# Recurrent units of a long mixed kernel take their buffers in two stages, and the gated branch runs in two threads

## The chip, the cores and the metric

The kernel runs on one core of a Trainium2 chip. Times are device microseconds (us) of one execution. A profile is one execution recorded by the hardware; its stretches and instructions are counted in us from the start of its span. The core has five instruction queues that matter here: TensorE (PE), VectorE (DVE), ScalarE (ACT), GpSimd (POOL), and SyncE (SP), which issues most transfers. Each works through its own instructions in the order in which the program holds them and waits where one of them needs a result of another engine.

## The reference, cut to what matters

Two blocks follow each other on a sequence of 1024 tokens with 1024 channels. The first is a two-layer transformer (pooling, sliding-window attention, two feed-forward networks). The second, which the change touches, computes

```
h = x*(1+scale) + shift;  p = h @ w_in                      # 29 column tiles of 128
out_a = u * (causal w_spatial @ layer_norm(v) + b) * silu(gate)   # per chunk of 128 tokens
r, k, v, w, a = token-shifted columns of p                  # 8 heads of 64
for t: S = S*w_t + (S a_t) b_t^T + v_t k_t^T;  y_t = S r_t  # RWKV-7
out_b = (group_norm(y) + bonus) * silu(gate)
x = layer_norm(ALPHA*x + gate*(concat(out_a, out_b) @ w_out))
```

## The kernel before, in words

Everything is FP32 in effect: a GEMM is done in three passes over a high and a low part (helper at L265, so every matmul has that line, and every transpose L269). The sequence is cut in two halves, h=0 and h=1. The program is written by generators ("threads") that a small planner runs: `yield 6000` lets other threads go on until a planned clock has moved on by that many ns, `("ev", x)` waits for an event, `("acq", pool, n)` for n buffers of a count. The planner's order is TensorE's order, word for word. On the other engines a scheduler orders the instructions by that order and by priorities.

The second block runs once for each half. While h=0 runs, the second feed-forward network of h=1 fills TensorE. In h=1 nothing else is left. `second` (L1384) makes 29 input GEMMs: one for the decay inputs (`wdad`), then k, r, v for four pairs of heads (`pk`, `pr`, `pv`), four gates (`pg`), and twelve for the gated branch (`pgv`, `pgu`, `pgg`). Their results take turns in four banks; ScalarE and VectorE copy each away, and it goes to memory.

A recurrent unit `rwkv(p, h)` (L1072) handles pair p of heads. Its names on TensorE, in order, are: `zw`, `za`, `kt`, `kn` (decays and norms of k), `A` (products inside chunks of 64, masked by VectorE into `Aa` and `W`), `bt`, `vt`, `bn`, `F`; then VectorE solves 16-by-16 triangles in 15 pairs of small instructions (L1182, L1183), with transfers through memory before (`nd`, `Dm`) and after (`ud`, `td`); then `P1`, `T3`, `U3`, `P2`, `U6` (larger triangles), `GH`, `QM`, eight steps of `S` (the state, one step after the other by way of ScalarE), `y`, and `yo` (transposes after the norm). In names as `zw2_1` the first digit is p and the second h. All small products share four more PSUM banks.

Buffers of 528 columns come from a pool of 67, counted by `T`. A unit takes 15 before it starts, gives 4 back after `GH`, 10 after `y`, and takes 3 for the norm. Two units can be under way at once in h=1. The gated branch (`gmlp`, L1012: `gc`, `gt`, `gp`) does its four blocks one after the other in one thread. `out_first` (L1420) projects h=0 (`po2`) and then normalizes it in its own thread of low priority by `final` (L1569: `mean0`, the squares' sum `sql0`, `st_ln0`, `sb_ln0`). `out_second` (L1447) projects h=1 in two halves of columns; its first three pieces (`po24`, `po26`, `po27`) do seven of the eight inputs before it needs unit 3.

Of the kernel before, what the change touches and what calls it, by code (L numbers as in the profile page):

```python
# [19 lines left out]
T = 1024  # L20
# [12 lines left out]
NT = 67  # L33
# [150 lines left out]
class K:  # L184
# [824 lines left out]
        nc.sync.dma_start(out=self.gd[h][which, m], in_=t)  # L1009
        self.events.add(n2)  # L1010

    def gmlp(self, h):  # L1012

        nc, rp = self.nc, self.rp
        for m in range(4):
            nm = f"{m}_{h}"
            yield ("ev", f"gv{m}{h}")
            yield ("ev", f"gu{m}{h}")
            yield ("ev", f"gg{m}{h}")

            wsp = rp.tile([128, 2, 128], F32, tag="wsp", name=f"wsp{nm}", bufs=1)
            self.load(wsp.rearrange("p e t -> p (e t)"), self.A["wsp"][:, 256 * m:256 * m + 256])
            nc.vector.tensor_tensor(out=wsp, in0=wsp, in1=self.caus.unsqueeze(1).to_broadcast([128, 2, 128]), op=ALU.mult)
            yield 6000
            pc = self.pss(f"gc{nm}")
            for e in range(2):
                self.mm(pc[64 * e:64 * e + 64, :128], self.ones[:, :64], wsp[:, e])
            C = rp.tile([128, 128], F32, tag="gC", name=f"gC{nm}", bufs=1)
            for e in range(2):
                self.load(C[64 * e:64 * e + 64, :], self.A["bsp"][2 * m + e:2 * m + e + 1, :].to_broadcast([64, 128]))  # L1030
            nc.vector.scalar_tensor_tensor(out=C, in0=pc[:, :128], scalar=self.v("lnv_b", m), in1=C, op0=ALU.mult, op1=ALU.add)
            yield ("acq", "TG"[h], 5)
# [12 lines left out]
            nc.vector.tensor_tensor(out=x3, in0=pv, in1=sm.unsqueeze(2).to_broadcast([128, 8, 64]), op=ALU.add)
            sq = self.tt(f"gq{nm}")
            nc.scalar.activation(out=sq, in_=xc, func=AF.Square)
            sm2 = self.tiny("gs2", f"gs2{nm}")
            nc.vector.reduce_sum(out=sm2, in_=sq.rearrange("p (a d) -> p a d", d=64), axis=AX.X)
            nc.vector.tensor_scalar(out=sm2, in0=sm2, scalar1=1.0 / 64, scalar2=LN_EPS, op0=ALU.mult, op1=ALU.add)  # L1050
            rs = self.tiny("gr", f"gr{nm}")
            nc.gpsimd.tensor_tensor(out=rs, in0=sm2, in1=self.nhalf[:, :8], op=ALU.pow)
            nc.gpsimd.tensor_tensor(out=x3, in0=x3, in1=rs.unsqueeze(2).to_broadcast([128, 8, 64]), op=ALU.mult)
            yield 17000
            po = self.pss(f"gp{nm}")
            for j in range(4):
                for e in range(2):
                    self.mm(po[64 * e:64 * e + 64, 128 * j:128 * j + 128], xc[:, 128 * j + 64 * e:128 * j + 64 * e + 64], wsp[:, e])
            t = self.tt(f"gw{nm}")
            nc.vector.scalar_tensor_tensor(out=t.rearrange("p (a b) -> p a b", b=128), in0=po.rearrange("p (a b) -> p a b", b=128),  # L1060
                                           scalar=self.v("lnv_g", m), in1=C.unsqueeze(1).to_broadcast([128, 4, 128]), op0=ALU.mult, op1=ALU.add)
            for x in (0, 2):
                u = self.tt(f"gl{nm}_{x}")
                self.after(nc.sync.dma_start(out=u, in_=self.gd[h][x, m]))
                nc.vector.scalar_tensor_tensor(out=t, in0=u, scalar=0.5 if x else 1.0, in1=t, op0=ALU.mult, op1=ALU.mult)
            nc.sync.dma_start(out=self.od[h][m], in_=t)
            yield 6000
            self.res["TG"[h]] += 5
            self.events.add(f"od{m}_{h}")
            yield 0  # L1070

    def rwkv(self, p, h):  # L1072
# [8 lines left out]
        yield ("ev", f"rk{nm}")  # L1081
        if h:
            yield ("ev", f"st{p}")
        yield ("acq", "early", 1)
        yield ("acq", "T", 15)
        k, r, v, wd = tl("k"), tl("r"), tl("v"), tl("wd")
        for t, m in ((wd, 16), (k, 4 + p), (r, p), (v, 8 + p)):
            self.after(nc.sync.dma_start(out=t, in_=self.qd[h][m]))
# [32 lines left out]
            self.tp(pn[:, 128 * j:128 * j + 128], sq[:, 128 * j:128 * j + 128])  # L1121
        kk = sq
        nc.vector.scalar_tensor_tensor(out=kk, in0=k, scalar=self.v("k_k", p), in1=pn, op0=ALU.mult, op1=ALU.mult)
        yield ("acq", "AR", 1)
        AR = rp.tile([128, 2, 512], F32, tag="AR", name=f"AR{nm}", bufs=3)
        BK = [tl(f"BK{par}_", 4, 2, 64) for par in range(2)]
        E3, k3 = c64(E), c64(kk)
        Aa3 = c64(AR[:, 0])
        nc.vector.scalar_tensor_tensor(out=Aa3[:, :, 1:64], in0=k3[:, :, 1:64], scalar=-1.0, in1=E3[:, :, 0:63], op0=ALU.mult, op1=ALU.mult)
        nc.vector.tensor_scalar(out=Aa3[:, :, 0:1], in0=k3[:, :, 0:1], scalar1=-1.0, scalar2=None, op0=ALU.mult)  # L1130
        nc.gpsimd.tensor_tensor(out=AR[:, 1], in0=r, in1=E, op=ALU.mult)
# [17 lines left out]
        Wc = lambda e, c: W[e][c // 4][:, c % 4]  # L1149
        ms = self.m64[:, 0:64].unsqueeze(1)  # L1150
        mi = self.m64[:, 64:128].unsqueeze(1)
        A4 = AR.rearrange("p s (c t) -> p s c t", t=64)
        for g in range(2):
            pq = [self.pss(f"A{nm}_{g}{e}") for e in range(2)]
            for e in range(2):
                for j in range(4):
                    c = 4 * g + j
                    pe = slice(64 * e, 64 * e + 64)
                    self.mm(pq[e][:, 128 * j:128 * j + 128], BK[c % 2][pe, c // 2].rearrange("p s t -> p (s t)"), A4[pe, :, c])
            for e, ps in enumerate(pq):  # L1160
                p4 = ps.rearrange("p (c r x) -> p r c x", r=2, x=128)
                for par in range(2):
# [124 lines left out]
        for g in range(2):  # L1287
# [8 lines left out]
            for par in range(2):  # L1296
                b = slice(64 * par, 64 * par + 64)
                for j in range(2):
                    nc.vector.tensor_copy(HV[par][b, hi(par, 2 * g + j)], p4[b, j, :, 64:128])
        self.res["T"] += 4  # L1300
        yield 2200

        QM = [tl(f"QM{par}_", 4, 128) for par in range(2)]
        for par in range(2):
# [3 lines left out]
            for cp in range(4):  # L1308
                for e in range(2):
                    self.mm(p3[64 * e:64 * e + 64, cp], G[b, cp, e], Wc(e, 2 * cp + par)[b])  # L1310
            nc.vector.tensor_tensor(out=QM[par][:, :, 0:64], in0=p3[:, :, 0:64], in1=pc(AR[:, 1])[:, :, par], op=ALU.add)
            nc.vector.tensor_tensor(out=QM[par][:, :, 64:128], in0=p3[:, :, 64:128], in1=self.m64[:, 192:256].unsqueeze(1).to_broadcast([128, 4, 64]), op=ALU.add)
        yield 1500

# [24 lines left out]
        for c in range(8):  # L1339
# [4 lines left out]
            for e in range(2):  # L1344
                pe = slice(64 * e, 64 * e + 64)
                self.mm(py[e][b, 64 * cp:64 * cp + 64], QM[par][pe, cp, 0:64], S[pe, c], False, True)
        self.res["T"] += 10
        self.res["S"] += 1
        self.res["AR"] += 1

        yield ("acq", "T", 3)
        y8 = self.tiny("y8", f"y8{nm}").rearrange("p (c e) -> p c e", e=2)
        yt = self.tt(f"yt{nm}")
        y4 = yt.rearrange("p (c e i) -> p c e i", e=2, i=64)
# [26 lines left out]
        self.res["T"] += 4  # L1381
        self.events.add(f"od{4 + p}_{h}")

    def second(self, h, X):  # L1384
        yield ("ev", f"x{X['name']}_0")
        if h:
            self.res["T"] += 14
            self.res["G"] = 5
        yield from self.shifted(16, h, X, f"wdad{h}")
        self.spawn(self.gmlp(h))  # L1390
        for p in range(4):
            self.spawn(self.rwkv(p, h), 2 - 0.01 * (4 * h + p))
            for n2, m in (("k", 4 + p), ("r", p), ("v", 8 + p)):
                yield from self.shifted(m, h, X, f"{n2}{p}{h}")
            self.events.add(f"rk{p}_{h}")
        for p in range(4):
            yield from self.shifted(12 + p, h, X, f"g{p}{h}")
            self.events.add(f"rg{p}_{h}")
        for x, m in ((1, 0), (0, 0), (2, 0), (1, 1), (0, 1), (2, 1), (1, 2), (0, 2), (2, 2), (1, 3), (0, 3), (2, 3)):
            yield from self.gmlp_gemm(x, m, h, X)  # L1400
        self.res["T"] += 16


    def cut(self, t, name):
# [12 lines left out]
    def out_first(self):  # L1417
# [259 lines left out]
```

## Time and profile before

| | |
|---|---|
| three runs | 2799.4, 2804.0 (median), 2806.66 us |
| the profiled execution | 2798.96 us, span 2797.2 us |
| TensorE busy | 2612.4 us, 93% of the span |
| VectorE, ScalarE, GpSimd busy | 1585.8, 1067.2, 347.0 us |
| mean granted clock of TensorE | 0.957 |

The granted clock says which part of its full 2.4 GHz TensorE ran at; 0.5 is the low level of 1.2 GHz. Busy time that overlaps between engines is no sum of the span. A wait names the instruction that was waited for.

### The profile page before, as it was taken

The page shows a single profiled execution, that of the slowest core. Times are in us where ns is not written, and L with a number is a line of the kernel's source. Part 1 is how long each engine was busy: PE and PEld are TensorE (multiplying, and loading weights), DVE is VectorE, ACT ScalarE, POOL GpSimd, SP SyncE. Part 2 cuts the span into 40 slices and gives each one's busy share as a digit, 9 for nine tenths or more (in the row PEclk, how much of TensorE's full clock was granted, in tenths as well). Part 3 has the DMA queues.
Part 4 walks back from the last instruction along what each step waited for, and adds up shares of the span by engine and source line. Part 5 has one row for each costly group of instructions (what it writes and reads, how often), then busy time and mean ns, then how long its engine had stood idle before and what let it go on. Part 6 is the DMA issues. An engine that isn't in the chain of part 4 may idle for free. (4 is left out here: it accounts for less than half of the span.)

```text
span 2797.2 us, 41641 instructions
## 1 busy us (share of the span) xinstructions
PE 2612.4 (93%) x16381; PEld 2172.6 (78%) x16381; DVE 1585.8 (57%) x3092; ACT 1067.2 (38%) x2009; POOL 347.0 (12%) x324
## 2 busy tenths in 40 slices
PE   5999999999999999999999999999999999997476
PEld 4988999888878877887888778777777777775366
DVE  6546654664665366545654655356675465645734
ACT  5333322354554333444543343333222234333223
POOL 3103000300000023000002111011020012104213
PEclk8999999999999999999999999999999999997668
DMA  4465343333222344222224344433233245432222
GB/s 148 131 144 174 129 136 91 128 116 101 90 74 76 106 147 130 92 96 81 81 87 128 114 137 136 134 103 117 86 100 100 96 144 178 126 128 90 86 71 68
DMA packets 183508, 314.57 MB, mean 112 GB/s; under 512 B 44792, under 2 KB 99498, under 8 KB 183312
## 3 DMA queue, kind: packets, MB, share of 16 engines
q1 hardware_dynamic: 174416, 296.06, 33.1%
q10 hardware_dynamic: 8896, 15.84, 2.4%
q8 instruction: 129, 2.11, 0.3%
q14 instruction: 67, 0.55, 0.1%
HBM read 266.60 MB, written 45.23 MB: 111 GB/s over the span
## 5 line engine op out<-in xcount | busy, mean ns | idle before, releaser
L265 PE MATMUL pda0A<-hha0A,wh_da0A 128*128 128x264 f32 x352 | 103.3, 293 | 10.9 <-ACT acca0A L646 6.8
L265 PE MATMUL po<-oc,wh_wo 128*128 128x256 f32 (+1 forms) x384 | 96.1, 344 | 13.1 <-ACT oc L1408 11.1
L265 PE MATMUL pga0A<-xh_a0A,wh_ga0A 128*128 128x264 f32 x352 | 102.9, 292 | 3.7 <-ACT xh_a0A L438 2.5
L265 PE MATMUL pda0A<-hla0A,wh_da0A 128*128 128x264 f32 x352 | 102.5, 291 | 1.0 <-DVE hla0A L637 1.0
L265 PE MATMUL pga0A<-xl_a0A,wh_ga0A 128*128 128x264 f32 x352 | 101.9, 289 | 0.5 <-DVE xl_a0A L439 0.5
L265 PE MATMUL pda0A<-hha0A,wl_da0A 128*128 128x264 f32 x352 | 102.3, 291 | 0.0
L265 PE MATMUL pua0A<-xh_a0A,wh_ua0A 128*128 128x264 f32 x352 | 102.2, 290 | 0.0
L265 PE MATMUL pua0A<-xh_a0A,wl_ua0A 128*128 128x264 f32 x352 | 101.4, 288 | 0.0
L265 PE MATMUL pua0A<-xl_a0A,wh_ua0A 128*128 128x264 f32 x352 | 101.4, 288 | 0.0
L265 PE MATMUL pga0A<-xh_a0A,wl_ga0A 128*128 128x264 f32 x352 | 101.4, 288 | 0.0
L392 POOL TENSOR_TENSOR sqo<-sqo,sq 128x512 f32<-128x512 f32 x4 | 5.2, 1294 | 743.7 <-ACT sq L391 743.7
L265 PEld LDWEIGHTS po<-oc,wh_wo 128*128 128x128 f32 x384 | 69.8, 207 | 21.9 <-ACT oc L1408 12.0
L817 ACT ACTIVATE l<-l,anm 128x256 f32<-128x256 f32 x128 | 63.5, 497 | 54.5 <-DVE anm L809 54.5
L265 PEld LDWEIGHTS pda0A<-hha0A,wh_da0A 128*128 128x128 f32 x352 | 68.7, 195 | 13.4 <-ACT acca0A L646 7.1
L265 PE MATMUL pda1B<-hha1B,wh_da1B 128*128 128x512 f32 x176 | 73.4, 417 | 3.4 <-DVE fg L632 2.4
L265 PE MATMUL pga1A<-xh_a1A,wh_ga1A 128*128 128x512 f32 x176 | 70.9, 403 | 2.2 <-ACT xh_a1A L464 2.2
L265 PE MATMUL pua1B<-xh_a1B,wh_ua1B 128*128 128x512 f32 x176 | 72.2, 410 | 0.0
L265 PE MATMUL pga1B<-xh_a1B,wh_ga1B 128*128 128x512 f32 x176 | 71.3, 405 | 0.8 <-ACT xh_a1B L464 0.6
L265 PE MATMUL pga1B<-xl_a1B,wh_ga1B 128*128 128x512 f32 x176 | 70.4, 400 | 1.7 <-DVE xl_a1B L465 1.7
L265 PEld LDWEIGHTS pga0A<-xh_a0A,wh_ga0A 128*128 128x128 f32 x352 | 67.8, 193 | 5.2 <-ACT xh_a0A L438 3.0
L265 PE MATMUL pda1A<-hha1A,wh_da1A 128*128 128x512 f32 x176 | 70.6, 401 | 1.1 <-ACT hha1A L636 1.1
L265 PE MATMUL pga1A<-xl_a1A,wh_ga1A 128*128 128x512 f32 x176 | 70.0, 398 | 1.6 <-DVE xl_a1A L465 1.6
(798 smaller groups left out, 8303.0 us busy)
## 6 DMA issues: line engine op xcount, KB each, us to landing
ada<-in_w_ada_dram ACTq DMA_DIRECT2D x24, 512.0 KB, 3.6
wr_ga0A<-in_wgu_dram SPq DMA_DIRECT2D x22, 512.0 KB, 4.1
wr_ua0A<-in_wgu_dram SPq DMA_DIRECT2D x22, 512.0 KB, 4.6
wr_da0A<-in_wdn_dram SPq DMA_DIRECT2D x22, 512.0 KB, 3.7
wr_ga0B<-in_wgu_dram SPq DMA_DIRECT2D x22, 512.0 KB, 3.5
wr_ua0B<-in_wgu_dram SPq DMA_DIRECT2D x22, 512.0 KB, 3.5
wr_da0B<-in_wdn_dram SPq DMA_DIRECT2D x22, 512.0 KB
wr_ga1A<-in_wgu_dram SPq DMA_DIRECT2D x22, 512.0 KB, 3.5
```

Source lines behind the costliest of these rows:

```text
L265: self.last = self.nc.tensor.matmul(out, lhsT, rhs, start=start, stop=stop).ins
L392: (eng or nc.gpsimd).tensor_tensor(out=acc[:, :w], in0=acc[:, :w], in1=sq[:, :w], op=ALU.add)
L817: nc.scalar.activation(out=lf[:, x], in_=lf[:, x], func=AF.Exp, bias=nm4[:, x:x + 1], accum_out=den[:, x:x + 1])
```

## The change

A unit now takes 10 buffers before it starts, 5 more when its triangles begin, gives 5 back after `GH`, 7 after `y`, and keeps 3 for the norm (given back at its end); there is no third wait for buffers. Its array `AR` is two tiles (halves of the sequence), so that the masks' inputs are written, multiplied and added by halves; there are six such tiles for three units, and unit 3 of h=1 takes its two from the pool of 67 instead. The pool's counts are larger in h=1. The gated branch keeps its two constant arrays in one buffer of the pool, and in h=1 its blocks 0, 2 and 1, 3 run in two threads. The gates' GEMMs (`pg`) no longer precede the gated branch's but alternate with them. The first half's last norm is a thread of its own with the usual priority.

```diff
-    def gmlp(self, h):
+    def gmlp(self, h, ms=range(4)):
...
-            wsp = rp.tile([128, 2, 128], F32, tag="wsp", name=f"wsp{nm}", bufs=1)
+            yield ("acq", "TG"[h], 6)
+            wc = self.ht(f"wsp{nm}")
+            wsp = wc[:, :256].rearrange("p (e t) -> p e t", e=2)
...
+        own = h == 1 and p == 3
         yield ("acq", "early", 1)
-        yield ("acq", "T", 15)
+        yield ("acq", "T", 12 if own else 10)
...
+            yield ("acq", "AR", 1)
+            AR = [rp.tile([128, 2, 4, 64], F32, tag="AR", name=f"AR{g}_{nm}", bufs=6) for g in range(2)]
...
+        yield ("acq", "T", 5)
         Un, Tn = tl("U"), tl("T")
...
-        self.res["T"] += 4
+        self.res["T"] += 5
...
-        self.res["T"] += 10
+        self.res["T"] += 9 if own else 7
...
-        yield ("acq", "T", 3)
...
         if h:
-            self.res["T"] += 14
-            self.res["G"] = 5
+            self.res["T"] += NT - 41
+            self.res["G"] = 6
...
-        self.spawn(self.gmlp(h))
+        if h:
+            for e in range(2):
+                self.spawn(self.gmlp(h, range(e, 4, 2)))
+        else:
+            self.spawn(self.gmlp(h))
...
         for p in range(4):
+            for x in (1, 0, 2):
+                yield from self.gmlp_gemm(x, p, h, X)
             yield from self.shifted(12 + p, h, X, f"g{p}{h}")
...
-        for x, m in ((1, 0), (0, 0), (2, 0), (1, 1), (0, 1), (2, 1), (1, 2), (0, 2), (2, 2), (1, 3), (0, 3), (2, 3)):
-            yield from self.gmlp_gemm(x, m, h, X)
-        self.res["T"] += 16
+        if h:
+            self.res["T"] += 10
+            self.res["G"] += 6
+        else:
+            self.res["T"] += 16
...
-        yield from self.final(y, 0, 512, ysum)
-        self.res["T"] += 12
+        self.spawn(self.final(y, 0, 512, ysum, 12))
```

TensorE, where unit 2 of h=1 starts. Before, `zw2_1` stands after unit 0's `yo`, with one GEMM (`pgg31`, the last of the 29) still to come:

```order
L265 MATMUL QM1_1_1_22739<-W00_1_1_21714,T1_1_21751 64x128
...
L269 MATMUL yo0_1_22750<-eye_75,yt0_1_22634 128x128 x4
L265 MATMUL zw2_1_22761<-wd2_1_22680,wup2_1_22685 128x512
L265 MATMUL za2_1_22762<-wd2_1_22680,wup2_1_22685 128x512
L269 MATMUL kt2_1_22781<-eye_75,kq2_1_22687 128x128 x4
...
L265 MATMUL gc1_1_22800<-wsp1_1_22689,ones_76 64x128 x2
L265 MATMUL pgg31_22818<-xh_b1B_0_0_20496,wh_gg31_22813 128x512
...
L269 MATMUL kn2_1_22849<-eye_75,kq2_1_22687 128x128 x4
```

Now it stands right after unit 1's `F`, among unit 0's triangles:

```order
L265 MATMUL F1_1_1_21947<-HV1_1_1_21930,Aa1_1_1_21808 64x64 x2
...
L265 MATMUL zw2_1_22076<-wd2_1_21972,wup2_1_21977 128x512
L265 MATMUL za2_1_22077<-wd2_1_21972,wup2_1_21977 128x512
L269 MATMUL kt2_1_22096<-eye_75,kq2_1_21979 128x128 x4
L265 MATMUL P20_1_22107<-T0_1_21401,Aa0_0_1_21362 32x32
...
L265 MATMUL gc0_1_22126<-wsp0_1_21985,ones_76 64x128 x2
L265 MATMUL pgv11_22148<-xh_b1B_0_0_20516,wh_gv11_22143 128x512
...
L265 MATMUL U60_1_22173<-U0_1_21400,N0_1_21571 32x32 x16
L269 MATMUL kn2_1_22192<-eye_75,kq2_1_21979 128x128 x4
```

Unit 2 moved from behind the 28th GEMM to behind the 17th; between its `kt` and `kn` there are `P2`, `gc`, one GEMM and `U6`.

TensorE, at the end of h=1. Before, unit 3's `P1` follows unit 2's `y`, and pieces of the output projection (`po2`) lie between unit 3's stages:

```order
L265 MATMUL S2_1_7_23763<-S2_1_23701,QM1_2_1_23669 64x64 x2
L265 MATMUL y2_1_0_23769<-HV0_2_1_23092,W00_2_1_22960 64x64
...
L265 MATMUL P13_1_23819<-T3_1_23395,N3_1_23572 64x64 x16
L265 MATMUL gp3_1_23838<-wsp3_1_23631,gx3_1_23729 64x128 x8
L265 MATMUL T33_1_23856<-P3_1_23836,U3_1_23394 64x64 x16
...
L265 MATMUL GH3_1_1_24043<-F1_3_1_23492,U3_1_23394 64x128 x8
L265 MATMUL po24_1_0_24066<-oc00_1_22895,wh_wo24_1_23966 128x256
...
L265 MATMUL QM3_1_0_24090<-W00_3_1_23358,T3_1_23395 64x128
...
L265 MATMUL po26_1_0_24112<-oc00_1_22895,wh_wo26_1_23972 128x256
...
L265 MATMUL S3_1_0_24136<-HV0_3_1_23478,W00_3_1_23358 64x64
...
L265 MATMUL y3_1_0_24206<-HV0_3_1_23478,W00_3_1_23358 64x64
...
L269 MATMUL yo3_1_24256<-eye_75,yt3_1_24241 128x128 x4
```

Now unit 3's `P1` comes one step after the last GEMM (`pg31`), beside unit 2's `S`:

```order
L265 MATMUL pg31_23659<-xh_b1B_0_0_20516,wh_g31_23654 128x512
...
L265 MATMUL S2_1_0_23686<-HV0_2_1_22494,W00_2_1_22360 64x64
...
L265 MATMUL P13_1_23692<-T3_1_23039,N3_1_23292 64x64 x16
L265 MATMUL S2_1_1_23734<-HV1_2_1_22495,W00_2_1_22360 64x64
...
L265 MATMUL T33_1_23740<-P3_1_23709,U3_1_23038 64x64 x16
...
L265 MATMUL GH3_1_1_23902<-F1_3_1_23136,U3_1_23038 64x128 x8
...
L265 MATMUL y2_1_0_23928<-HV0_2_1_22494,W00_2_1_22360 64x64
...
L265 MATMUL QM3_1_0_23980<-W00_3_1_22988,T3_1_23039 64x128
...
L265 MATMUL S3_1_0_24006<-HV0_3_1_23122,W00_3_1_22988 64x64
...
L265 MATMUL y3_1_0_24171<-HV0_3_1_23122,W00_3_1_22988 64x64
...
L265 MATMUL po24_1_0_24230<-oc00_1_23724,wh_wo24_1_24102 128x256
...
L269 MATMUL yo3_1_24296<-eye_75,yt3_1_24206 128x128 x4
```

The pieces of the output projection moved behind unit 3's `y`.

VectorE, the first half's last norm. Before, its subtractions and its sum of squares stand among the masks of unit 2 (`Aa`, `W`):

```order
L1008 SCALAR_TENSOR_TENSOR sgg31_22889<-sgg31_22889,pgg31_22818 128x512
...
L1579 TENSOR_TENSOR yo20_0_20506<-yo20_0_20506,mean0_22901 128x512
...
L1579 TENSOR_TENSOR yo26_0_20789<-yo26_0_20789,mean0_22901 128x512
L1163 TENSOR_TENSOR Aa0_2_1_22958<-A2_1_00_22964,m64_14001 128x128
...
L1164 TENSOR_TENSOR W00_2_1_22960<-A2_1_00_22964,m64_14001 128x4x64
L392 TENSOR_TENSOR sql0_22903<-sql0_22903,sq_22931 128x512
L1163 TENSOR_TENSOR Aa0_2_1_22958<-A2_1_01_22965,m64_14001 128x128
```

Now they stand in front of the first copies of h=1's GEMM results (`shwdad1`, `shk01`):

```order
L330 TENSOR_TENSOR wl_v01_21006<-wr_v01_21004,wh_v01_21005 128x1024
L1593 TENSOR_TENSOR yo20_0_20526<-yo20_0_20526,mean0_20893 128x512
...
L1593 TENSOR_TENSOR yo26_0_20809<-yo26_0_20809,mean0_20893 128x512
L392 TENSOR_TENSOR sql0_20895<-sql0_20895,sq_20923 128x512
L985 SCALAR_TENSOR_TENSOR shwdad1_20926<-pwdad1_20866,vecs_74,shwdad1_20926 128x511
L987 TENSOR_TENSOR shwdad1_20926<-shwdad1_20926,shp_14011 128x1
L985 SCALAR_TENSOR_TENSOR shk01_20963<-pk01_20938,vecs_74,shk01_20963 128x511
```

The sum of squares, which waits for GpSimd, moved out of unit 2 and ahead of the units altogether.

## Rows read from the trace of the kernel before

**Rows 1.** The page's head, and its row of the granted clock in 40 slices.

```profile
span 2797.2 us, 41641 instructions
...
PEclk8999999999999999999999999999999999997668
```

**Rows 2.** Two stretches of h=1: length, busy time by engine (instructions), clock, DMA.

```profile
core 0: us, PE busy (x) PEld busy (x) DVE busy (x) ACT busy (x) POOL busy (x), PEclk, DMA share, GB/s
2327.45:2541.25 213.80, 212.39 (x1515) 167.78 (x1515) 116.44 (x269) 78.22 (x121) 27.50 (x27) 1.00 0.42 134
2541.25:2731.80 190.55, 112.30 (x1165) 87.94 (x1165) 96.97 (x246) 51.48 (x104) 45.34 (x40) 0.66 0.25 76
```

**Rows 3.** Stretches: A to F; F; P; P2; T, U; GH; QM; y; S step.

```profile
2385.32:2391.16 5.84, 5.84 (x53) 4.86 (x53) 3.35 (x14) 2.20 (x6) 2.02 (x2) 1.00 0.06 7
2396.89:2398.01 1.12, 1.12 (x33) 1.05 (x32) 0.00 (x0) 0.59 (x1) 0.00 (x0) 1.00 0.86 310
2436.01:2437.26 1.25, 1.25 (x33) 1.19 (x32) 0.31 (x1) 0.00 (x0) 0.60 (x1) 1.00 0.29 32
2451.61:2452.23 0.62, 0.62 (x34) 0.58 (x33) 0.62 (x2) 0.62 (x1) 0.00 (x0) 1.00 0.00 0
2494.71:2496.67 1.96, 1.96 (x68) 1.89 (x66) 0.69 (x1) 0.53 (x2) 0.99 (x1) 1.00 0.43 146
2464.37:2466.26 1.89, 1.89 (x33) 1.72 (x33) 1.03 (x3) 0.98 (x2) 0.00 (x0) 1.00 0.20 18
2472.01:2473.53 1.52, 1.52 (x33) 1.35 (x32) 0.00 (x0) 0.03 (x1) 0.00 (x0) 1.00 0.99 383
2518.17:2523.02 4.85, 4.85 (x64) 3.84 (x63) 0.00 (x0) 0.00 (x0) 0.00 (x0) 1.00 0.95 321
2479.66:2480.19 0.53, 0.53 (x10) 0.40 (x9) 0.00 (x0) 0.42 (x1) 0.00 (x0) 1.00 0.86 224
```

**Rows 4.** Timeline of TensorE at zw to kn of unit 1.

```profile
2403.77 0.69 PE L265 MATMUL zw<-wd,wup 64*128 64x512 f32 x1
...
2404.83 0.65 PE L269 MATMUL kt<-eye,kq 128*128 128x128 f32 x4
2405.24 0.48 PE L265 MATMUL pv<-xh_b1B,wh_v 128*128 128x512 f32 x1
...
2417.91 0.63 PE L269 MATMUL kn<-eye,kq 128*128 128x128 f32 x4 [1.30 <-DVE kq L1117]
```

**Rows 5.** Waits of TensorE from 2541 to 2732: us in total, times, longest.

```profile
PE S L265 <- DVE QM L1312: 6.9, 2, 5.0
...
PE bt L269 <- DVE W L1164: 3.4, 1, 3.4
```

**Rows 6.** Stretches at a gap before the first half's output projection.

```profile
2272.00:2276.00 4.00, 0.30 (x2) 0.00 (x0) 2.56 (x5) 2.58 (x4) 1.26 (x1) 0.93 1.04 394
2276.00:2286.00 10.00, 8.38 (x23) 6.66 (x24) 6.58 (x12) 3.75 (x8) 1.94 (x1) 0.52 0.27 104
```

**Rows 7.** Timeline of TensorE: P and yo of unit 3, output projection.

```profile
2670.47 0.37 PE L265 MATMUL P<-T,N 64*64 64x64 f32 x1
...
2722.33 1.08 PE L269 MATMUL yo<-eye,yt 128*128 128x128 f32 x4 [5.83 <-DVE yt L1368]
2731.81 1.31 PE L265 MATMUL po<-oc,wh_wo 128*128 128x256 f32 x2 [8.40 <-ACT oc L1408]
```

**Rows 8.** Stretches of the output projection's first three pieces alone.

```profile
2684.28:2692.87 8.59, 5.43 (x21) 4.22 (x21) 0.00 (x0) 0.00 (x0) 0.70 0.62 238
2695.70:2699.72 4.02, 4.02 (x21) 3.88 (x21) 0.00 (x0) 0.00 (x0) 0.63 0.70 235
2702.16:2706.34 4.18, 4.18 (x21) 4.04 (x21) 0.00 (x0) 0.00 (x0) 0.60 0.00 0
```

**Rows 9.** Timeline of VectorE among unit 2's masks.

```profile
2570.86 0.69 DVE L392 TENSOR_TENSOR sql<-sql,sq 128x512 f32<-128x512 f32 x1 [13.53 <-POOL sql L392]
```

More of the change, by code (lines that the diff above doesn't have):

```diff
@@ L1010, in gmlp_gemm @@
         self.events.add(n2)
-    def gmlp(self, h):
-        nc, rp = self.nc, self.rp
-        for m in range(4):
+    def gmlp(self, h, ms=range(4)):
+        nc = self.nc
+        for m in ms:
             nm = f"{m}_{h}"
@@ L1027, in gmlp @@
                 self.mm(pc[64 * e:64 * e + 64, :128], self.ones[:, :64], wsp[:, e])
-            C = rp.tile([128, 128], F32, tag="gC", name=f"gC{nm}", bufs=1)
+            C = wc[:, 256:384]
             for e in range(2):
@@ L1031, in gmlp @@
             nc.vector.scalar_tensor_tensor(out=C, in0=pc[:, :128], scalar=self.v("lnv_b", m), in1=C, op0=ALU.mult, op1=ALU.add)
-            yield ("acq", "TG"[h], 5)
             x = self.tt(f"gv{nm}")
@@ L1067, in gmlp @@
             yield 6000
-            self.res["TG"[h]] += 5
+            self.res["TG"[h]] += 6
             self.events.add(f"od{m}_{h}")
@@ L1123, in rwkv @@
         nc.vector.scalar_tensor_tensor(out=kk, in0=k, scalar=self.v("k_k", p), in1=pn, op0=ALU.mult, op1=ALU.mult)
-        yield ("acq", "AR", 1)
-        AR = rp.tile([128, 2, 512], F32, tag="AR", name=f"AR{nm}", bufs=3)
+        if own:
+            AR = [tl(f"AR{g}_", 2, 4, 64) for g in range(2)]
+        else:
+            yield ("acq", "AR", 1)
+            AR = [rp.tile([128, 2, 4, 64], F32, tag="AR", name=f"AR{g}_{nm}", bufs=6) for g in range(2)]
         BK = [tl(f"BK{par}_", 4, 2, 64) for par in range(2)]
         E3, k3 = c64(E), c64(kk)
[L1128 to L1131, printed above, removed]
+        for g in range(2):
+            c = slice(4 * g, 4 * g + 4)
+            nc.vector.scalar_tensor_tensor(out=AR[g][:, 0, :, 1:64], in0=k3[:, c, 1:64], scalar=-1.0, in1=E3[:, c, 0:63], op0=ALU.mult, op1=ALU.mult)
+            nc.vector.tensor_scalar(out=AR[g][:, 0, :, 0:1], in0=k3[:, c, 0:1], scalar1=-1.0, scalar2=None, op0=ALU.mult)
+            nc.gpsimd.tensor_tensor(out=AR[g][:, 1], in0=c64(r)[:, c], in1=E3[:, c], op=ALU.mult)
         pcol = rp.tile([128, 8], F32, tag="pcol", name=f"pcol{nm}", bufs=3)
@@ L1151, in rwkv @@
         mi = self.m64[:, 64:128].unsqueeze(1)
-        A4 = AR.rearrange("p s (c t) -> p s c t", t=64)
         for g in range(2):
@@ L1158, in rwkv @@
                     pe = slice(64 * e, 64 * e + 64)
-                    self.mm(pq[e][:, 128 * j:128 * j + 128], BK[c % 2][pe, c // 2].rearrange("p s t -> p (s t)"), A4[pe, :, c])
+                    self.mm(pq[e][:, 128 * j:128 * j + 128], BK[c % 2][pe, c // 2].rearrange("p s t -> p (s t)"), AR[g][pe, :, j])
             for e, ps in enumerate(pq):
@@ L1225, in rwkv @@
             for j in range(2):
-                self.tp(p4[:, j, :, 0:64], AR[:, 0, 128 * (2 * g + j):128 * (2 * g + j) + 128])
+                self.tp(p4[:, j, :, 0:64], AR[g][:, 0, 2 * j:2 * j + 2].rearrange("p c t -> p (c t)"))
             pf.append((ps, p4))
@@ L1310, in rwkv @@
                     self.mm(p3[64 * e:64 * e + 64, cp], G[b, cp, e], Wc(e, 2 * cp + par)[b])
-            nc.vector.tensor_tensor(out=QM[par][:, :, 0:64], in0=p3[:, :, 0:64], in1=pc(AR[:, 1])[:, :, par], op=ALU.add)
+            for g in range(2):
+                c = slice(2 * g, 2 * g + 2)
+                nc.vector.tensor_tensor(out=QM[par][:, c, 0:64], in0=p3[:, c, 0:64], in1=AR[g][:, 1, par::2], op=ALU.add)
             nc.vector.tensor_tensor(out=QM[par][:, :, 64:128], in0=p3[:, :, 64:128], in1=self.m64[:, 192:256].unsqueeze(1).to_broadcast([128, 4, 64]), op=ALU.add)
@@ L1346, in rwkv @@
                 self.mm(py[e][b, 64 * cp:64 * cp + 64], QM[par][pe, cp, 0:64], S[pe, c], False, True)
-        self.res["T"] += 10
+        self.res["T"] += 9 if own else 7
         self.res["S"] += 1
-        self.res["AR"] += 1
-        yield ("acq", "T", 3)
+        self.res["AR"] += not own
         y8 = self.tiny("y8", f"y8{nm}").rearrange("p (c e) -> p c e", e=2)
@@ L1380, in rwkv @@
         yield 6000
-        self.res["T"] += 4
+        self.res["T"] += 3
         self.events.add(f"od{4 + p}_{h}")
@@ L1396, in second @@
         for p in range(4):
+            for x in (1, 0, 2):
+                yield from self.gmlp_gemm(x, p, h, X)
             yield from self.shifted(12 + p, h, X, f"g{p}{h}")
             self.events.add(f"rg{p}_{h}")
-        for x, m in ((1, 0), (0, 0), (2, 0), (1, 1), (0, 1), (2, 1), (1, 2), (0, 2), (2, 2), (1, 3), (0, 3), (2, 3)):
-            yield from self.gmlp_gemm(x, m, h, X)
-        self.res["T"] += 16
+        if h:
+            self.res["T"] += 10
+            self.res["G"] += 6
+        else:
+            self.res["T"] += 16
     def cut(self, t, name):
@@ L1567, in tail_end, with final @@
         yield 0
-    def final(self, y, c0, n, ysum):
+    def final(self, y, c0, n, ysum, held=0):
         nc = self.nc
@@ L1584, in final @@
         self.ln_out(y, dg, c0, n)
+        self.res["T"] += held
     def ln_out(self, y, dg, c0, n):
```

## The prediction, as it was put on record

> **What bounds the kernel now.** I read the slices of the page first, then stretches of the end, then the waits of TensorE inside them, then single instructions. The page gives a span of 2797.2 us, and a granted TensorE clock of a full 10 tenths or close to it until the last four slices, where it reads 7, 6, 6 and 8 [rows 1]. So nearly the whole kernel is bound by TensorE, and only the end is not. Two stretches divide the second half of the sequence (h=1) at the end of its 29th and last input GEMM: from 2327.45 to 2541.25 us TensorE is busy 212.39 of 213.80 us at clock 1.00; from there to 2731.80, where the output projection gets its eighth input, it is busy 112.30 of 190.55 us at clock 0.66 [rows 2]. The reason is the order of work: when the GEMMs are used up, units 2 and 3 of the recurrent branch are still almost whole, and each is a long chain of small matmuls with vector work between them. The 65 us after 2731.8 (output projection and norm) are not touched by the change.
>
> **The sum.** The change moves no FLOPs; it moves matmuls of units 1, 2 and 3 in front of the last GEMM, where they fill TensorE between GEMMs, and leaves a shorter chain behind it. I therefore add up (a) the work that now stands before the end of the last GEMM, (b) the new waits there, (c) the chain from there to the eighth input.
>
> (a) Prices from dense stretches of units 0 and 1 at full clock [rows 3]: A to the first F matmuls 5.84, rest of F 1.12, P 1.25, P2 0.62 (U6 the same), T and U 1.96, GH 1.89, QM 1.52, y 4.85, one S step 0.53; the four transposes of kn 0.63, and zw, za, kt together 1.47 [rows 4]. By the order, these now precede the end of the last GEMM and did not before: of unit 2 everything from kn to QM, 5.84+1.12+1.25+1.96+2x0.62+1.89+1.52+0.63 = 15.5; of unit 3 from zw to F, 1.47+0.63+5.84+1.12 = 9.1; of unit 1 seven S steps, y and yo, 3.7+4.85+0.63 = 9.2; two blocks of the gated branch, about four and a half groups the size of kn, 2.7; the mean, sum and spread of the first half's norm, four such groups and a bit, 3. Sum 39 us. The last GEMM would end at 2541 + 39 = 2580 if TensorE never waited.
>
> (b) It will wait, because VectorE now has four units instead of two. VectorE is busy 116.44 us of the first stretch and 96.97 of the second [rows 2]: 213 us which must fit into about 340, a share of 0.63 instead of 0.53. Three waits can be priced. First kn: for unit 1 it came 12.4 us after kt (2405.48 to 2417.91), with two GEMMs of 5.69 us between, and still waited 1.30 us for kq [rows 4], because VectorE had unit 0's triangular solve in front of it. In the new order only one GEMM, P2, U6 and the gate's bias stand between kt and kn of unit 2, 7.3 us, and about 8.0 for unit 3; VectorE still has a solve in front in both cases. So 5.1 + 4.4 = 9.5 us. Second, the masks after A: bt of unit 2 waited 3.4 us for W in the old end, where A shared VectorE with something else [rows 5]; twice that, 6.8. Third, S waiting for QM's additions: 6.9 us in two waits [rows 5]; the additions are now also cut in halves; again 6.9. Sum 23 us. A gap of 4 us also cost the clock: in 2272 to 2276 TensorE did 0.30 us of work, and the next 10 us ran at 0.52 of full clock, the low level of 1.2 GHz [rows 6]. The two waits at kn are of that size: 4 us each, 8 in all. Together 31 us. Bounds: below 1.3 us, which is all that two units cost TensorE in the first stretch; above the 78 us idle (190.55 - 112.30) that the same stages left in the old end. I take 31, nearer the lower row, since GEMMs still stand between the stages. The last GEMM then ends at 2611.
>
> (c) Old chain: P of unit 3 at 2670.47 to the eighth input at 2731.81, 61.3 us [rows 7]. Out of it go three pieces of output projection that stood between GH, QM and S: 8.6, 4.0 and 4.2 us, 16.8 [rows 8]. Into it come unit 2's S steps beside unit 3's small products (seven, 5 us with their copies), y of unit 2 4.85, and the gate's last pieces, 2: 11.9. The three pieces now stand after y of unit 3 and before yo, 12.4 us at the price they had, of which 5.83 lie in yo's old wait [rows 7]; I take 5. So 61.3 - 16.8 + 11.9 + 5 = 61.4, and one S step before P: 62. No gain there; the S chain of unit 2 is what takes the room.
>
> Eighth input at 2611 + 62 = 2673 instead of 2731.8: 59 us earlier. The profiled execution took 2798.96 us for its span of 2797.2; minus 59 is 2740. The median of the three runs, 2804.0, stands 5 us above that execution; between the two I forecast **2742 us**.
>
> **Edits at nothing.** The early norm: VectorE's queue now has the first half's sum of squares ahead of the GEMM evacuations. In the old place that one addition kept VectorE idle 13.53 us for GpSimd [rows 9], in the middle of unit 2's masks. In the new place it holds up four evacuations; four banks take GEMM results, so a fifth GEMM is the first to wait, some 20 us later. Cover enough; if GpSimd takes twice as long, it costs up to 10 us. The same move takes the 13.53 us out of the worst place of the old end, which is part of the 59. The halves of AR add four VectorE instructions per unit, and the gate's constants move into the large pool: below 1 us per unit, under GEMMs. The first half (h=0) runs under feed-forward GEMMs that keep TensorE full, so its new order is worth between -2 and +2 us. SP: weights for later GEMMs now queue behind the solve's transfers and the loads of units 2 and 3, but each is issued at least one GEMM and several stages before use; I take 0, and up to 6 us for the last one, which stands behind unit 3's solve.
>
> **Rivals.** *Waits hardly grow* (b near 5 us): for it, 1.4 us of idle in 213.8 us of the first stretch; against it, kn's 1.30 with twice the distance. Gain 85, time 2716. *VectorE becomes the bound*, each stage of a unit waiting as in the old end (b near 78): for it the strict order on VectorE and four small PSUM banks for four units; against it a share of 0.63. Gain 12, time 2790. *Slower, by the clock*: if waits of 4 us recur between every two GEMMs, TensorE never leaves the low level. For it, the 10 us after one gap [rows 6] and 0.66 over the old end; against it, a GEMM of 5.7 us after most waits, and clock 1.00 throughout two overlapped units. From kn of unit 2 (about 2459) some 121 us of work would remain to 2580, at half speed 242: last GEMM at 2701 + 23 of waits = 2724, eighth input 2786, time 2798.96 + 54 = 2853, with the median's offset about 2855. It decides once some 60 us of added time are reached, that is half the stage at the low level. *It does not overlap*: buffers of unit 3 come free only when unit 0 is done; the order puts zw of unit 3 among unit 0's S steps, so the loads would have to wait. Then unit 3 stays behind, and the time is within 8 us of 2804.
>
> The Trainium skill bears on the clock rival: "TensorE: Matmul & The Clock Gate", section "HAM oscillation — how this bites in real kernels", says that a loop whose compute between waits is short is throttled again at every wait. By that rule the time would go to the rival's 2853. The rows on one gap agree; the dense GEMMs between the waits speak for recovery, as after 2286 us, where the clock is 1.00 again.
>
> **How the numbers follow.** Forecast, with (b) between 15 and 45: 0.55, own range 2726 to 2758. Waits hardly grow: 0.2. VectorE the bound: 0.17. Slower by the clock: 0.04. No overlap: 0.04. The range from 2712 to 2785 leaves out the last two and half of VectorE's case, and a tip of the best. About 0.3% (8 us) is what a measurement can tell from no change: faster 0.92, same 0.04, slower 0.04.
>
> **What would show it.** In the changed profile: the last GEMM ends near 2611 and not before 2580; TensorE is busy near 0.9 of the time from 2327 to there; kn of units 2 and 3 wait 4 to 5 us each for kq; P of unit 3 directly follows the last GEMM; about 60 us lie from there to the eighth input; sql0 no longer stands among the masks. The prediction is wrong if the last GEMM ends after 2640, if the clock between 2450 and 2600 averages below 0.8, or if the chain behind the last GEMM is longer than 75 us.

## The result, and the profile after

The changed kernel takes 2763.2 us in the median (2758.47 to 2765.6), the kernel before 2803.24: a ratio of 0.9855, with a 95% interval of 0.9836 to 0.9875, 40 us less. Forecast were 2742 in a range of 2712 to 2785. The profiled execution took 2765.6 us. Its page head and clock row, as [rows 1]:

```profile
span 2763.8 us, 41692 instructions
...
PEclk8999999999999999999999989999999999998978
```

The last four slices read 8, 9, 7, 8 where they read 7, 6, 6, 8. The stretches divide at the events of [rows 2], with one more in front and one behind: from the first GEMM of h=0 to that of h=1, from there to the end of the last GEMM, on to the eighth input, and the rest. The columns are length, then busy time of PE, PEld, DVE, ACT, POOL, clock, DMA share and GB/s.

```profile
1656.98:2339.55 682.57, 656.27 (x4149) 516.04 (x4148) 384.84 (x736) 217.88 (x330) 80.92 (x80) 0.98 0.36 114
2339.55:2623.74 284.19, 265.26 (x2089) 208.50 (x2089) 185.78 (x461) 110.02 (x181) 63.48 (x63) 0.94 0.39 122
2623.74:2698.00 74.26, 48.65 (x591) 39.40 (x592) 31.34 (x69) 22.49 (x47) 11.13 (x8) 0.74 0.36 118
2698.00:2763.80 65.80, 49.13 (x345) 45.80 (x345) 31.44 (x65) 21.19 (x51) 22.71 (x29) 0.84 0.19 60
```

Before, the first of these lasted 668.68 us:

```profile
1658.77:2327.45 668.68, 651.31 (x4150) 513.33 (x4149) 385.83 (x720) 217.78 (x330) 75.64 (x76) 0.99 0.37 116
```

So the h=0 stretch is 13.9 us longer (8.9 of them idle TensorE, 5.0 longer busy time) and h=1 starts 12.1 us later than before; its GEMM stretch of 284.19 us has the forecast length (2611 - 2327.45 = 283.55), and the chain behind it is 12.3 us longer than the 62 forecast. Both misses show in VectorE's queue. In h=0, S of unit 1 waits for QM:

```profile
1976.10 0.34 PE L265 MATMUL S<-HV,W 128*64 128x64 f32 x4
1985.54 0.48 PE L265 MATMUL S<-S,QM 64*64 64x64 f32 x4 [9.11 <-DVE QM L1320]
```

QM's additions are ready to run, but VectorE stands at a weight's low part (it waits 4.93 us for the high part) and at the gated branch's constants (2.02 us):

```profile
1977.87 1.22 DVE L330 TENSOR_TENSOR wl_ua1B<-wr_ua1B,wh_ua1B 128x1024 fp32r<-128x1024 f32 x1 [4.93 <-ACT wh_ua1B L329]
...
1983.64 0.43 DVE L1025 TENSOR_TENSOR wsp<-wsp,caus 128x256 f32<-128x256 f32 x1 [2.02 <-DMA wsp<-in_wsp_dram]
...
1984.59 0.48 DVE L1319 TENSOR_TENSOR QM<-QM,AR 128x128 f32<-128x128 f32 x2
```

Both came late: in SP's queue they stand behind the solve's transfers, the weight behind `ud` and `td` (no issue of SP's for 13.4 us before `ud`), the constants behind sixteen small ones.

```profile
1956.25 0.38 SPq L322 DMA_DIRECT2D wr_ga1B<-in_wgu_dram  x1
1970.05 0.48 SPq L1193 DMA_DIRECT2D ud<-Xm  x1
1970.58 0.59 SPq L1193 DMA_DIRECT2D td<-pd  x1
1971.26 0.54 SPq L322 DMA_DIRECT2D wr_ua1B<-in_wgu_dram  x1
1972.06 5.49 SPq L1198 DMA_DIRECT2D U<-ud  x8
1977.65 3.69 SPq L1198 DMA_DIRECT2D T<-td  x8
1981.43 0.37 SPq L276 DMA_DIRECT2D wsp<-in_wsp_dram  x1
```

At the end it is the norm of unit 3, whose third instruction (L1366) stands behind four inputs' low parts and eight weight parts, some waiting for loads:

```profile
2670.01 0.76 DVE L1364 TENSOR_REDUCE y<-y 128x4 f32<-128x256 f32 x2 [6.06 <-PE y L265]
2670.69 0.29 DVE L1365 TENSOR_SCALAR y<-y 128x4 f32<-128x4 f32 x2
2671.36 2.67 DVE L1424 TENSOR_TENSOR oc<-or,oc 128x512 fp32r<-128x512 f32 x4 [0.38 <-ACT oc L1423]
2673.94 2.49 DVE L330 TENSOR_TENSOR wl_wo<-wr_wo,wh_wo 128x512 fp32r<-128x512 f32 x4
2679.41 1.29 DVE L330 TENSOR_TENSOR wl_wo<-wr_wo,wh_wo 128x512 fp32r<-128x512 f32 x2 [2.98 <-ACT wh_wo L329]
2682.45 1.29 DVE L330 TENSOR_TENSOR wl_wo<-wr_wo,wh_wo 128x512 fp32r<-128x512 f32 x2 [1.75 <-ACT wh_wo L329]
2683.66 0.75 DVE L1366 TENSOR_TENSOR yt<-y,y 128x256 f32<-128x256 f32 x2
```

From y of unit 3 (its end at 2669.98) to the eighth input (2698.00) it takes 28.0 us:

```profile
2669.65 0.33 PE L265 MATMUL y<-S,QM 64*64 64x64 f32 x4
...
2688.59 1.08 PE L269 MATMUL yo<-eye,yt 128*128 128x128 f32 x4 [9.07 <-DVE yt L1375]
2698.00 1.30 PE L265 MATMUL po<-oc,wh_wo 128*128 128x256 f32 x2 [8.33 <-ACT oc L1423]
```

Before, it took 15.3, to be read from [rows 7] and this row:

```profile
2716.17 0.33 PE L265 MATMUL y<-S,QM 64*64 64x64 f32 x4
```

All of the difference lies between y and `yo`: 18.6 us instead of 5.8.

### The profile page after: what moved, and what is told of

Same layout as the page of the kernel before. It is cut to its first block, busy times and chain, and to the rows that moved or that the text cites. A ratio compares the mean times of both kernels' runs of the same rounds, so it can differ in the third digit from the quotient of the medians.

```text
span 2763.8 us, 41692 instructions
## 1 busy us (share of the span) xinstructions
PE 2604.0 (94%) x16381; PEld 2162.8 (78%) x16381; DVE 1586.6 (57%) x3124; ACT 1070.2 (39%) x2012; POOL 355.1 (13%) x332
## 5 line engine op out<-in xcount | busy, mean ns | idle before, releaser
L265 PE MATMUL pda0B<-hha0B,wh_da0B 128*128 128x512 f32 x176 | 70.5, 400 | 1.1 <-ACT hha0B L636 1.1
```

Source lines behind the costliest of these rows:

```text
L265: self.last = self.nc.tensor.matmul(out, lhsT, rhs, start=start, stop=stop).ins
```

## The experiments

Ratios are to the kernel before, run on the same chip at the same time (its medians were 2802.89 to 2805.16). "h=0 stretch" (us from the first GEMM of h=0 to that of h=1) and "y to eighth" (us from the end of y of unit 3 to the eighth input) are read from each run's profile.

| run | median us | ratio, 95% interval | h=0 stretch | y to eighth |
|---|---|---|---|---|
| the change | 2763.2 | 0.9855 [0.9836, 0.9875] | 682.6 | 28.0 |
| e1_norm3 | 2759.86 | 0.9849 [0.9829, 0.9868] | 681.2 | 23.9 |
| e2_old_first_half | 2750.56 | 0.9819 [0.9799, 0.9838] | 672.6 | 27.5 |
| e3_late_norm | 2775.72 | 0.9901 [0.9884, 0.9917] | 682.6 | 15.3 |
| e4_before_early_norm | 2754.5 | 0.9824 [0.9804, 0.9844] | 669.3 | 26.8 |
| e5_early_norm_held | 2786.42 | 0.9937 [0.9922, 0.9953] | 672.3 | 15.3 |
| e6_units_staged_only_in_h0 | 2762.84 | 0.9857 [0.9841, 0.9872] | 682.8 | 27.9 |
| e7_tail | 2750.51 | 0.981 [0.9792, 0.9829] | 674.8 | 22.3 |
| e8_before_early_norm_tail | 2752.67 | 0.9821 [0.9804, 0.9838] | 674.3 | 25.5 |
| e9_tail_in_order | 2741.22 | 0.9769 [0.975, 0.9789] | 672.3 | 17.0 |
| e10_tail_and_sum_on_gpsimd | 2736.7 | 0.9764 [0.9744, 0.9783] | 675.5 | 17.0 |
| e11_staged_h1_late_norm | 2766.64 | 0.9861 [0.9847, 0.9875] | 675.3 | 15.4 |
| e12_before_early_norm_tail_sum | 2741.45 | 0.9786 [0.9771, 0.9802] | 668.8 | 20.2 |

**Which part of the change gains the time.** The kernel before, e4, e11 and e2 make a square of the early norm and the staged buffers (with the larger counts and the second thread of the gated branch, which no run takes apart); e3 and e5 stand beside it.

```diff
 # e3: the change, norm late          # e4: before, with the spawn alone
-        self.spawn(self.final(y, 0, 512, ysum, 12))
+        yield from self.final(y, 0, 512, ysum, 12)
 # e5: e4, but the 12 buffers are given back at y of unit 1 (one line of it)
+        self.res["T"] += 22 if (p, h) == (1, 1) else 10
 # e11: e3 with the first half as in e2
```

> The changed kernel with the first half's last norm back in the low-priority thread of its projection, everything else as changed. Theory A (what the early norm is worth is that it gives 12 buffers back early, so that unit 3 can start among the S steps of unit 0): zw of unit 3 comes only after QM of unit 1, the last GEMM ends some 10 us earlier but the chain behind it is 20 to 30 longer, time 2770 to 2785. Theory B (the early norm only costs the 6.5 us by which the first six GEMMs of h=1 are later): time 2755 to 2759.

> The kernel before with one part of the change alone: the first half's last norm is a thread of its own with the usual priority and gives its 12 buffers back early. Theory A (the buffers that this norm held are what kept units 2 and 3 back, taking buffers in two stages adds little): units 2 and 3 start among the GEMMs as in the changed kernel, the first half is as before, time 2750 to 2768. Theory B (taking buffers in two stages is what lets four units run): units 2 and 3 stay behind the last GEMM or nearly so, time 2795 to 2815.

> The kernel before with the first half's norm early as in the last experiment, but its 12 buffers are counted free only after y of unit 1 of h=1, about where the late norm gave them back. It tells apart what the early norm does: Theory A (the 12 buffers are what let units 2 and 3 start early): zw of unit 2 is again behind y of unit 0, the gain is gone but for the norm's own place, time 2785 to 2802. Rival (the gain comes from taking the norm's VectorE and GpSimd work out of the end): time 2753 to 2770.

> Buffers in two stages, larger pool and gated branch in two threads in h=1 as changed, the first half as before, and the norm late as before: the change without the early norm and without its cost in the first half. With the kernel before, e4_before_early_norm (early norm alone) and e2_old_first_half (both) it completes a square. Theory (both parts do the same thing, they give units 2 and 3 their buffers earlier): 10 to 13 us below e3_late_norm, 2762 to 2766, so that staging alone gains about 40, the early norm alone 49, both 53. Rival (the two add up): 2790 to 2800.

The times bear out theory A in e3, e4 and e5, and the theory of e11 within 1 us of its range. The stages of e3 were less well foreseen: its last GEMM ends 26 us earlier than in the change, not 10, and the chain behind it is 37 us longer, not 20 to 30. The early norm alone (e4) gains 49 us, more than the whole change. Its two stages of h=1, to the last GEMM and on to the eighth input:

```profile
2326.78:2590.07 263.29, 253.91 (x2061) 200.23 (x2060) 176.38 (x428) 108.47 (x180) 57.00 (x55) 0.99 0.40 127
2590.07:2681.85 91.78, 55.09 (x621) 44.84 (x618) 43.01 (x89) 23.50 (x48) 16.96 (x11) 0.69 0.34 109
```

With the buffers held until the old place (e5), zw of unit 2 is again behind y of unit 0, and 32 of the 49 us are lost:

```profile
2545.20 0.69 PE L265 MATMUL zw<-wd,wup 64*128 64x512 f32 x1
```

```profile
2329.49:2553.57 224.08, 218.25 (x1529) 171.16 (x1529) 131.21 (x285) 88.34 (x139) 43.53 (x37) 0.98 0.42 137
2553.57:2719.19 165.62, 103.48 (x1153) 82.30 (x1152) 85.23 (x230) 40.55 (x86) 30.25 (x30) 0.70 0.25 75
```

Counted from the first GEMM of h=1, units 2 and 3 start (zw) after 205 and 266 us before, after 216 and 259 in e5, but after 129 and 211 in e4, 118 and 202 in e11, 128 and 178 in the change. So mostly the count of buffers decides when units 2 and 3 may start; the other 17 us of the early norm come without it. The staging gives them buffers too: without the early norm, and with the old first half, it gains 38 (e11). Both together gain 53 (e2), not 49 + 38, and the intervals of e2 and e4 overlap: beside the early norm no gain of the staging is shown.

**The first half.** e2 restores the old rules in h=0, e6 only those of the gates and the gated branch.

```diff
 # e2, one line of it; e6 leaves this line as changed
-        yield ("acq", "T", 12 if own else 10)
+        yield ("acq", "T", 15 if h == 0 else 12 if own else 10)
```

> The changed kernel, but in the first half (h=0) the units take 15 buffers at once and give back 4 and 10 as before, the gate GEMMs precede the gated branch's, and the gated branch keeps its constants in tiles of its own and takes 5 buffers later, all as before; h=1 as in the changed kernel. Theory (the new order of the first half cost 13.9 us between the first GEMM of h=0 and the first of h=1, 682.6 against 668.7): that stretch is back to 668 to 671 us, time 2749 to 2753. Rival (the loss comes from the larger number of half-width instructions on VectorE and not from the order): the stretch stays above 678, time 2759 to 2764.

> The changed kernel, but in the first half only the gate GEMMs and the gated branch are as before; the units of h=0 still take their buffers in two stages. Theory (in h=0 a unit that starts 18 us earlier pushes transfers in front of weight loads on SP, and VectorE then waits for weight casts ahead of QM): the stretch from the first GEMM of h=0 to that of h=1 stays at 679 to 684 us, time 2759 to 2764. Rival (the interleaved gates and the gated branch's constants cost it): the stretch is 670 to 674, time 2749 to 2753.

The theory held in both, but for the stretch of e2 (672.6 us, 668 to 671 expected). Four profiles with the new order of units have 681.2 to 682.8 us in the h=0 stretch, ten with the old one 668.7 to 675.5: about 10 us. In e6 the wait for QM is down to 1.3 us and others stand in its place (yo 4.3, kn 4.5), at the same idle time (26.8 us, 26.3 in the change). So it is not that one wait. What e6 shares with the change, and e2 does not, is that the units of h=0 take their buffers in two stages and unit 2 starts earlier: its zw comes 241 us after the first GEMM of h=0 in the change and 238 in e6, but 258 before and 261 in e2. Which queue costs how much stays open.

**The end.** e1 plans the norm of unit 3 ahead of inputs 3 to 6 and the last weights; e7 (on e2) and e8 (on e4) also put yo ahead of the three pieces; e9 moreover puts unit 3's product ahead of the last weights, on VectorE and on SP.

```diff
 # out_second; "n3_1" comes after the norm, "t3_1" after yo (e7 to e10, e12)
+            if k == 3:
+                yield ("ev", "n3_1")
...
+            if i == 4:
+                yield ("ev", "t3_1")
 # split_weight of the last four (e9, e10, e12): low part after unit 3's product
+                    self.after(lo, self.lastq)
```

> The changed kernel with one edit: the output projection's inputs 3 to 6 and its last four weights are planned only after the last unit's norm, so on VectorE the five instructions of that norm stand in front of the four low parts and eight weight parts instead of behind them. Theory (the chain behind the last GEMM was 12 us longer than forecast because the norm queued behind work that waits for weight loads): from the end of y of unit 3 to yo falls from 18.6 us to 6 to 9, the eighth input comes 10 to 13 us earlier, time 2750 to 2753. Rival (the weights and inputs are then what is late, the projection waits for them instead): time 2760 to 2764, with a new wait of po for oc or for the weights behind y.

> The kernel of the experiment with the old first half, and at the end the last unit's norm stands first: inputs 3 to 6 are planned after the norm, yo directly follows y on TensorE, the last four weights and the three first pieces of the output projection come behind yo. Theory (the chain behind the last GEMM is too long by the norm's wait on VectorE and by pieces in front of yo): from the end of y of unit 3 to the eighth input 16 to 20 us instead of 28, time 2739 to 2744. Rival (the pieces are then what is late and nothing is won, as they no longer lie beside the norm): 22 to 28 us, time 2746 to 2752.

> The kernel before with the early norm alone and the same order at the end as in e7_tail. Theory: y of unit 3 to the eighth input 16 to 20 us instead of 26.8, time 2744 to 2748. Rival: 22 to 27 us, time 2750 to 2756.

> As e7_tail (units of h=0, gates and gated branch of h=0 as before), and moreover the last unit's product with its gate stands ahead of the last weights' parts on VectorE, its way through memory ahead of the last two weight loads on SP. In e7_tail that product came 4 us after GpSimd was done and the transfer to memory took 5.1 us beside 1 MB of weights. Theory: y of unit 3 to the eighth input 15 to 17 us (22.3 in e7_tail, 15.3 in the kernel before), time 2743 to 2747. Rival (the two weights are now late for the projection): as much idle time appears behind the eighth input, time 2749 to 2755.

In e1, e7 and e8 the theory failed and the time is that of the rival (for e1 at its edge): each time the wait moved on. In e1 yo stood behind pieces that waited 4.7 us for the inputs' high and low parts; in e7 the product's way through memory took 5.1 us beside 1 MB of weights (issued at 2674.93, the load behind it at 2680.03), and as long in e8:

```profile
2673.12 1.54 SPq L322 DMA_DIRECT2D wr_wo<-in_wout_dram  x2
2674.93 0.33 SPq L1397 DMA_DIRECT2D od<-yq  x1
2680.03 0.33 SPq L1445 DMA_DIRECT2D or<-od  x1
```

In e9 this takes 2 us, and the eighth input comes 17.0 us after y, with less than 1 us of waiting for it on TensorE:

```profile
2668.17 0.32 SPq L1399 DMA_DIRECT2D od<-yq  x1
2670.22 0.32 SPq L1447 DMA_DIRECT2D or<-od  x1
...
2673.70 0.38 PE L265 MATMUL po<-oc,wh_wo 128*128 128x256 f32 x1 [0.65 <-ACT oc L1441]
```

So e9 is 9 us below e2, clear of its interval and 2 us below the expected range; the intervals of e1, e7 and e8 overlap those of their bases (the change, e2 and e4).

**The price of the early norm, and a version without staging.**

```diff
-            self.sq_add(sq, x, n, i == 0, nc.vector if i == KT - 1 else None)
+            self.sq_add(sq, x, n, i == 0, nc.vector if i == KT - 1 and c0 else None)
```

> As e9_tail_in_order, with one instruction moved: the last of the seven additions of squares of the first half's norm (sql0) is GpSimd's instead of VectorE's, so that VectorE need not wait for GpSimd ahead of the evacuations of the first GEMMs of h=1. Theory (of the 6.5 us by which zw of unit 0 is later than before, 3 to 5 are that wait): from the first GEMM of h=1 to zw of unit 0 about 36 us instead of 40, time 3 to 5 us below e9_tail_in_order. Rival (the banks would have covered it, the delay is the norm's own matmuls and its spread): no change within 1 us.

> The kernel before with the early norm, the order at the end and the sum of squares of e10_tail_and_sum_on_gpsimd, without buffers in two stages, the larger pool counts and the second gate thread. It tells what these are worth when the rest is equal. Theory (nothing, since the 12 buffers already let units 2 and 3 start early): within 6 us of e10_tail_and_sum_on_gpsimd, 2733 to 2743. Rival (they matter once the end is in order, since the GEMMs there end 19 us earlier and leave a longer chain): 2745 to 2755.

In e10 zw of unit 0 comes 38.7 us after the first GEMM instead of 39.8 in e9: the rival (within 1 us) was right on the place. The median is 4.5 us lower, which the overlapping intervals do not settle. e12 agrees with its theory: without staging the time is 2741.45, and the interval overlaps that of e10. Both beat the change and the kernel before, clear of their intervals.

## Why the prediction was right, and where it was wrong

The direction and the range held; of the 62 us forecast 40 came. In the profiled pair the forecast was 2740 and 2765.6 was measured, 25.6 more: 12.1 by the late start of h=1, 0.6 in the GEMM stretch, 12.3 in the chain, 0.4 behind it, the rest rounding. Of the signs named, the last GEMM (2623.74, bound 2640) and the clock (0.92, bound 0.8) are well inside; the chain (74.3) is just under its bound of 75.

**(a) and (b), moved work and new waits:** 70 us were forecast, 70.4 measured (284.19 - 213.80), with terms that cancel, so the hit is in part luck. TensorE was idle 18.9 us (284.19 - 265.26), not 24.4 (23, and 1.4 as before): kn waits 4.4 in all, not 9.5, and no S in the stretch waits for QM, but yo of unit 1 waits 4.9 and GH 3.3, which the sum left out.

```profile
PE yo L269 <- DVE yt L1375: 4.9, 1, 4.9
PE kn L269 <- DVE kq L1119: 4.4, 3, 1.9
PE GH L265 <- DVE HV L1305: 3.3, 1, 3.3
PE bt L269 <- DVE W L1169: 2.9, 1, 2.9
PE sb_ln L269 <- DVE dg_ln L367: 2.4, 1, 2.4
```

TensorE was busy 13.9 us longer than the 251.4 that the old 212.39 and (a) make at full clock (8 forecast). The low clock accounts for it: 30.1 us of the busy time ran at 0.50, and at full clock the same work would take half of that, 15 us less (an estimate). More than half of the 30.1 lies in one place; one of four shorter falls stands below it:

```profile
2529.30:2549.80 20.50, 16.53 (x111) 13.00 (x112) 12.96 (x36) 4.45 (x9) 1.67 (x4) 0.50 0.26 66
2607.82:2611.20 3.38, 3.38 (x12) 2.43 (x13) 2.23 (x10) 1.27 (x2) 1.28 (x1) 0.50 0.05 21
```

**Edits at nothing, first half, -2 to +2 us:** this step failed. It reasoned that full GEMMs hide a new order. The start of h=1 moved by 12.1 us in this pair (the stretch by some 10 over all profiles), and e2 and e6 put it on the units of h=0 that take their buffers in two stages. That it comes about in the queues of SP and VectorE, which carry GEMM weights and the units' work alike, is read from the one wait above and not tested. That the first half was a bystander was assumed, and no row was read for it.

**Edits at nothing, early norm:** cover by four banks was argued, with up to 10 us if it fails. From the first GEMM (2327.45 before, 2339.55 now) to zw of unit 0 it is 40.0 us instead of 33.5, and 6.5 is more than the 3 of work in (a):

```profile
2360.97 0.69 PE L265 MATMUL zw<-wd,wup 64*128 64x512 f32 x1
```

```profile
2371.88 0.72 PE L269 MATMUL sb_ln<-eye,dg_ln 128*128 128x128 f32 x4 [2.39 <-DVE dg_ln L367]
...
2379.56 0.69 PE L265 MATMUL zw<-wd,wup 64*128 64x512 f32 x1
```

The banks did cover: TensorE's one wait in these 40 us is that of 2.39 us for the norm's spread, no GEMM waits, and in e10, with the addition moved away, 1.1 us came back. More important, the step treated as a side issue what alone gains 49 us: the 12 buffers that the norm holds were not counted. The stages' order was taken from the changed program as a whole, so the time came out right without its cause.

**(c), the chain:** 62 forecast, 74.3 measured. Of this 45.9 us are P to y of unit 3 (41 to 42 by the sum) and 28.0 y to the eighth input (20.3 by the sum: 15.3 and 5). The 4 us more up to y of unit 3 are the size of one term: y of unit 2, priced 4.85 at full clock, took 9.2 (2640.87 to 2650.08), with the clock at 0.50 from 2641.94. The 5 us for the three pieces assumed that they lie in yo's old wait; nothing was counted for the weights and inputs that now stand ahead of the norm on VectorE. e9 shows the size: 10.5 us less between y and the eighth input than in e2, 9 us less in time.

**Rivals:** VectorE as the bound (2790) and the low clock (2855) did not come, nor did waits that hardly grow (b came to 31.4 us) or no overlap (zw of unit 3 is at 2517.85, ahead of the last GEMM). The mean clock was 0.94 in the GEMM stretch and 0.92 from 2450 to 2600. The rule quoted from the Trainium skill ("TensorE: Matmul & The Clock Gate", section "HAM oscillation — how this bites in real kernels") is that short compute between waits is throttled again at every wait. The trace agrees as to the falls: in the GEMM stretch, each of the five longest waits that began at full clock (before `sb_ln` 2.39 us, `bt` 2.90, `kn` 1.91 and 1.84, `yo` 4.94) came with a fall to 0.50 within 1 us of its end. But four of these falls lasted only 3.4 us. The fifth, the 20.5 us above, began at this wait and ran through y of unit 0, with a further wait of 3.33 us at `GH`, into the next GEMM:

```profile
2529.64 1.08 PE L269 MATMUL kn<-eye,kq 128*128 128x128 f32 x4 [1.84 <-DVE kq L1119]
```

So the clock fell at the waits, as the rival had it, but came back, and the low level took 34 of the 284 us.

## What to carry to other kernels

When a change has several parts, run each alone: here one line alone gains more than the whole, and the part in the title, which alone gained 38 us with the old first half, showed no gain beside it and cost some 10 us in the first half. Ask who holds the buffers for which the late work waits: a norm that nobody needs early can be worth moving for what it gives back. In these queues an instruction that waits for a load holds up all that stands behind it (QM's additions above), and mending one such wait pays only when the next one in the chain is mended too.

## What the runs showed of the hardware

VectorE and GpSimd slowed each other. The norm's five subtractions on VectorE took 3.09 us in the kernel before, where GpSimd's three ran later and took 3.71:

```profile
2553.52 3.09 DVE L1579 TENSOR_TENSOR yo<-yo,mean 128x512 f32<-128x512 f32 x5
```

```profile
2559.19 3.71 POOL L1579 TENSOR_TENSOR yo<-yo,mean 128x512 f32<-128x512 f32 x3
```

In the changed kernel they ran side by side:

```profile
2346.86 8.65 DVE L1593 TENSOR_TENSOR yo<-yo,mean 128x512 f32<-128x512 f32 x5 [2.19 <-ACT mean L1590]
```

```profile
2346.83 4.72 POOL L1593 TENSOR_TENSOR yo<-yo,mean 128x512 f32<-128x512 f32 x3 [3.25 <-ACT mean L1590]
2351.51 9.25 POOL L392 TENSOR_TENSOR sql<-sql,sq 128x512 f32<-128x512 f32 x6
```

That is 1.73 us for one on VectorE instead of 0.62, and 1.57 for one on GpSimd instead of 1.24; e4, e5, e9 and e12 show the same (8.6 to 8.7 us for the five). Whether the early norm's 6.5 us would be fewer without it, no run tests. The Trainium skill ("SBUF — State Buffer", section "SBUF: two separate sides") says that the two engines share a pair of ports, which a VectorE instruction with two inputs in SBUF and a GpSimd instruction that reads SBUF cannot use together: the one that starts first holds it for its whole instruction while the other waits. The trace agrees: one of each in turn would be 0.62 + 1.24 = 1.86 us by the rows of the kernel before, near the 1.73.
